# Gate stretch of a PEER layer: gathered rows a group later, weight copies behind the activation that frees their buffer, later splits behind a block's first product

## The chip, the cores and the metric

The program runs on one core of a Trainium2 chip. The metric is the device time of one execution in microseconds (us). Five engines of the core work side by side, each through its own queue in a fixed order: PE (matrix products; PEld is its weight load), DVE (vector work), ACT (activations and copies), POOL (here: indirect DMAs that gather table rows) and SP (it only issues DMAs). An engine waits at the head of its queue until what that instruction needs is there; nothing behind it can pass.

## The reference

Two layers over a sequence of 512 tokens of width 1024: a Griffin-like recurrent mixer in layer 0, latent attention in layer 1, and in both layers the same channel mixer, PEER, in which the change lies:

```python
def peer(h, w_q, sub_keys, u_tab, v_tab):
    q = (h @ w_q).reshape(B, S, PEER_HEADS, 2, PEER_HALF)
    s = jnp.einsum('bshpd,hpnd->bshpn', q, sub_keys)
    ...                                  # top 16 of 16 x 16 candidates per head
    idx = e1 * N_KEYS + e2               # 8 heads x 16 experts of 16384 per token
    g = jax.nn.softmax(cv, axis=-1)
    act = jax.nn.gelu(jnp.einsum('bcd,bchkd->bchk', hc, u_tab[ic]), approximate=False)
    return jnp.einsum('bchk,bchkd->bcd', gc * act, v_tab[ic])
```

## The kernel before

The 512 tokens are four blocks of 128. For the first three blocks (384 tokens) the kernel computes all 16384 experts densely and multiplies with a gate matrix that is zero where a token did not choose an expert. Only for the fourth block it gathers the 128 chosen rows per token one by one. Matrices in f32 are split into a high and a low part, and three products of the parts are added (`mm3`, lines 216 to 218).

Work comes in four kinds of pieces:

- A **u-part** (`u_part`, 128 in each layer, one per 128 experts): SP loads 512 KB of the u table (`raw`, four buffers), ACT copies it to `whi` (L179, three buffers), DVE subtracts to get `wlo` (L180), PE runs 24 products into one of two accumulator banks `u`, ACT applies the gelu (L1145 and L1140, `gact` or `gsp`) and, where `gsp` is written to memory, issues the store (L1141). The gelu is what frees the bank for the u-part after the next.
- A **gate group** (`gate_group`, 24 in each layer: 8 for each of three blocks, 16 tokens a group) is two half-groups. DVE makes two one-hot tensors `oo` (L1041) and the product `pr` of one of them with the gate (L1043, two buffers each); PE runs 16 products per half-group into `wps`; ACT copies `wps` to `stg` (L1052, two copies a half-group) and stores the group to `wscr` (L1054).
- A **gathered row** (`gather_steps`, 256 in each layer, in batches of 16 of the u table and then 16 of the v table): POOL gathers 512 KB into `grow` (four buffers), DVE makes a scalar product with it (L1487, `gdot`) or adds it to `gacc` (L1492).
- **Decoding** (`decode`, small `oh` work on DVE, some copies `ib` on ACT): it makes the gates of the next block, 7 steps in 8 groups.

After the choice of experts comes the **gate stretch**: 15 u-parts, and then 24 gate groups with some 2.5 u-parts for each group, and 74 gathered rows (`EARLY`) spread over groups 0 to 19. Then seven u-parts, and the products with the v table (`acc`), which read the gates back.

What stands where in a queue is settled when the program is built: a scheduler orders the instructions of all engines by a timeline of its own, unless the code says more. `issue_after(x)` says more: what the block issues on x's engine stands in the queue behind x. It adds no wait of its own, and it binds only instructions on that one engine. The loop that the change touches reads, before:

```python
for i in range(nt):
    more = 1 if i >= nsg and i % nsg < nsg // 2 else 0
    while state["u"] < n0 + (LEAD - UEND - n0) * (i + 1) // nt + more:
        u_part(after=wlast[-2])
    w, p = self.gate_group(pool, l, i // nsg, i % nsg, *prep[i // nsg])
    ...
    with tc.issue_after(plast[max(0, i - 1)]):
        while done < min(EARLY, EARLY * (i + 1) // (nt - QUIET)):
            next(gsteps)
            done += 1
```

Here `nt` is 24, `nsg` 8, `QUIET` 4 and `LEAD` 93.

Of the kernel before, what the change touches and what calls it, by code (L numbers as in the profile page):

```python
# [15 lines left out]
AF = mybir.ActivationFunctionType  # L16
OP = mybir.AluOpType
# [6 lines left out]
KC = D // P  # L24
# [15 lines left out]
ND = 3 * P  # L40
NSG = ND // TG
RING = 20
SPILL = 66
OWN = KC * T // ND
LEAD = OWN + RING - 3 + SPILL
# [3 lines left out]
QUIET = 4  # L49
EARLY = 74  # L50
# [5 lines left out]
GSCALE = 16384.0  # L56
# [27 lines left out]
class Trunk:  # L84
# [940 lines left out]
        nc.vector.tensor_tensor(gp[:, :, 1], gt, gp[:, :, 0], op=OP.subtract)  # L1025
        return et, gp

    def gate_group(self, pool, l, b, sg, et, gp):
        nc = self.nc
        shp = [P, 2, HT, P // 2, 2]  # L1030
        io = self.iota_e[:, 0].rearrange("p (e d) -> p e d", d=2).unsqueeze(1).unsqueeze(1).to_broadcast(shp)
        by_pair = "p q t (e d) -> p q t e d"
        stg = pool.tile([P, P, TG], F32, name="stg", bufs=2)
        for t0 in range(0, TG, HT):

            def toks(ap):
                return ap[:, (sg * TG + t0) // HT].unsqueeze(3).to_broadcast(shp)

            oo = pool.tile([P, 2, HT, P], F16, name="oo", bufs=2)
            pr = pool.tile([P, 2, HT, P], F16, name="pr", bufs=2)  # L1040
            nc.vector.tensor_tensor(oo.rearrange(by_pair, d=2), io, toks(et), op=OP.is_equal)  # L1041
            hot = oo[:, 0].rearrange("p t (e d) -> p t e d", d=2).unsqueeze(1).to_broadcast(shp)
            prod = nc.vector.tensor_tensor(pr.rearrange(by_pair, d=2), hot, toks(gp), op=OP.mult)  # L1043
            for a in range(0, HT, 4):
                wps = self.bank("wps")
                for t in range(4):
                    w = oo[:, 1, a + t]
                    out = wps[:, t * P:t * P + P]
                    lead = nc.tensor.matmul(out, w, pr[:, 0, a + t], start=True, stop=False).ins  # L1049
                    last = self.follow(lead, out, w, pr[:, 1, a + t], stop=True)  # L1050
                c = t0 + a
                nc.scalar.activation(stg[:, :, c:c + 4].rearrange("p e t -> p t e"),  # L1052
                                     wps.rearrange("p (t e) -> p t e", t=4), AF.Copy, scale=1.0 / GSCALE)
        nc.scalar.dma_start(self.wscr[l, b * (P // TG) + sg], stg.rearrange("p e t -> p (e t)"))  # L1054
        return last.ins, prod.ins

    def peer(self, l):
        nc, io, tc = self.nc, self.io, self.tc
        nd = NB - 1
        with ExitStack() as st:  # L1060
# [19 lines left out]
            with own:  # L1080
                for i, hs in enumerate(HALVES):
                    for k in range(KC):
# [5 lines left out]
                        hi, lo = (p[:, hs] for p in h[k])  # L1088
# [31 lines left out]
            gact, state = {}, {"u": 0}  # L1120

            def ring(t):
                held = (t - OWN) % RING < RING - 3
                return acts.tile([P, ND], F32, name="gact" if held else "gsp", bufs=RING - 3 if held else 3)

            nc.scalar.dma_start(self.xscr, self.x)

            def u_part(after=None, eng=None):
                t = state["u"]
                state["u"] = t + 1  # L1130
                out = self.bank("u", True)
                hi, lo = self.wtile(io["uT"][l][t], KC, eng=eng or nc.vector)
                with tc.issue_after(after) if after is not None else ExitStack():
                    for k, (bh, bl) in enumerate(h):
                        self.mm3(out[:, :ND], (hi[:, k, :], lo[:, k, :]), (bh[:, :ND], bl[:, :ND]), k == 0, k == KC - 1)
                if t < OWN:
                    gact[t] = self.x.rearrange("p k t -> p (k t)")[:, t * ND:t * ND + ND]
                elif LEAD - SPILL <= t < LEAD:
                    g = acts.tile([P, ND], F32, name="gsp", bufs=3)
                    nc.scalar.activation(g, out[:, :ND], AF.Gelu)  # L1140
                    nc.scalar.dma_start(self.gscr[l, t - (LEAD - SPILL)], g)  # L1141
                    return
                else:
                    gact[t] = ring(t)
                nc.scalar.activation(gact[t], out[:, :ND], AF.Gelu)  # L1145

            gpool = st.enter_context(tc.tile_pool(name=f"gath{l}", bufs=1))
            dec = st.enter_context(ExitStack())
# [5 lines left out]
            done = 0  # L1154
            total = 2 * P
            prep, gsel, gsteps = {}, [], None
            dpool = dec.enter_context(tc.tile_pool(name=f"dec{l}", bufs=1))

            def decodes(bs):
                for b in bs:  # L1160
                    res = []
                    for _ in self.decode(dpool, cvs[b], cis[b], iu[b], res):
                        yield
                    if b == nd:
                        gsel.append(self.gather_index(gpool, l, *res))
                    else:
                        prep[b] = self.gate_prep(pool, *res)

            with tc.tile_pool(name=f"pq{l}", bufs=1) as pool:
# [12 lines left out]
                for grp in range(4):  # L1182
# [7 lines left out]
                    for m in range(4):  # L1190
                        if m >= len(outs):
                            outs.append(self.bank("pq"))
                            with tc.issue_after(first) if first is not None else ExitStack():
                                w = self.wtile(io["w_pq"][wq + m], KC, eng=nc.gpsimd if grp else nc.vector)
                            self.lin(outs[m], w, h)
                        q = pool.tile([P, T], F32, name="pq_s", bufs=5)
                        nc.scalar.activation(q, outs[m], AF.Copy)
                        qs.append(q)
                    for b in (nd, *range(nd)):
# [4 lines left out]
                        for m in range(4):  # L1204
                            last = self.topk_half(pool, sc[:, m * P:m * P + P], vs[b][:, 4 * grp + m, :],
                                                  iu[b][:, 4 * grp + m, :])
# [9 lines left out]
            with tc.tile_pool(name=f"gate{l}", bufs=1) as pool:  # L1216
                nsg = P // TG
                steps = decodes(range(nd))
                for i in range(UDEC):
                    u_part()  # L1220
                while 0 not in prep:
                    next(steps)
                n0, nt = state["u"], nd * nsg
                ds = 0
                wlast, plast = [None, None], []
                for i in range(nt):
                    more = 1 if i >= nsg and i % nsg < nsg // 2 else 0
                    while state["u"] < n0 + (LEAD - UEND - n0) * (i + 1) // nt + more:
                        u_part(after=wlast[-2])
                    w, p = self.gate_group(pool, l, i // nsg, i % nsg, *prep[i // nsg])  # L1230
                    wlast.append(w)
                    plast.append(p)
                    while ds < 7 * (i + 2) // nsg:
                        next(steps, None)
                        ds += 1
                    with tc.issue_after(plast[max(0, i - 1)]):
                        while done < min(EARLY, EARLY * (i + 1) // (nt - QUIET)):
                            next(gsteps)
                            done += 1
                while state["u"] < LEAD:  # L1240
                    u_part(after=wlast[-1])
# [136 lines left out]
            for t, pair in held:  # L1378
                last = v_part(t, 0, *pair)
            self.preload(AF.Sqrt, emit(0))  # L1380
            rest, c = None, 0
            for q in range(2):
                for i, (t, pair) in enumerate(held):
                    with tc.issue_after(last):
                        last = v_part(t, 1, *pair, 2 * q * P, 2 * P, rest)
# [3 lines left out]
                    for _ in range((0, 2, 1, 1, 1, 0)[LAST * q + i]):  # L1389
                        with tc.issue_after(last):  # L1390
                            last = finish(c)
# [196 lines left out]
```

## Time and profile before

| What | us |
| --- | --- |
| median of 3 runs (2929.94 to 4088.32) | 2935.42 |
| the profiled execution | 2935.3 |
| its span, first to last instruction | 2933.5 |
| PE busy in the span | 2868.5 |
| DVE busy | 2469.5 |
| ACT busy | 1424.2 |
| POOL busy | 1104.4 |

The gate stretch of layer 0 runs from about 424 to 742 us of the span, that of layer 1 from about 1928 to 2246 us. The profile counts an engine as busy from an instruction's start to its modelled end, so a busy PE need not run at its peak; products that follow each other overlap, and their pace is read from their starts. In a line of the timeline the first number is the start, the second the duration, and the bracket at the end tells how long the engine was idle before it and what ended that wait.

### The profile page before, as it was taken

The page shows a single profiled execution, that of the slowest core. Times are in us where ns is not written, and L with a number is a line of the kernel's source. Part 1 is how long each engine was busy: PE and PEld are TensorE (multiplying, and loading weights), DVE is VectorE, ACT ScalarE, POOL GpSimd, SP SyncE. Part 2 cuts the span into 40 slices and gives each one's busy share as a digit, 9 for nine tenths or more (in the row PEclk, how much of TensorE's full clock was granted, in tenths as well). Part 3 has the DMA queues.
Part 4 walks back from the last instruction along what each step waited for, and adds up shares of the span by engine and source line. Part 5 has one row for each costly group of instructions (what it writes and reads, how often), then busy time and mean ns, then how long its engine had stood idle before and what let it go on. Part 6 is the DMA issues. An engine that isn't in the chain of part 4 may idle for free.

```text
span 2933.5 us, 43947 instructions
## 1 busy us (share of the span) xinstructions
PE 2868.5 (98%) x15680; PEld 2561.6 (87%) x15680; DVE 2469.5 (84%) x4717; ACT 1424.2 (49%) x2103; POOL 1104.4 (38%) x865
## 2 busy tenths in 40 slices
PE   7999999999999999999999999999999999999998
PEld 5688999999888889998778789999999888899997
DVE  8987899997988888879878877899986777888888
ACT  5754556665433333333576753556654333333333
POOL 4008715432232234535434446235321111245542
PEclk9999999999999999999999999999999999999999
DMA  8535559999999999999323343479999999999996
GB/s 314 189 137 186 169 179 370 355 368 339 327 372 360 367 315 354 322 348 324 113 87 130 122 137 124 138 282 356 369 344 335 314 330 317 317 329 353 349 334 218
DMA packets 296220, 813.71 MB, mean 277 GB/s; under 512 B 33153, under 2 KB 130561, under 8 KB 289601
## 3 DMA queue, kind: packets, MB, share of 16 engines
q1 hardware_dynamic: 188928, 439.41, 43.3%
q0 software_dynamic: 78912, 287.34, 27.5%
q10 hardware_dynamic: 28160, 84.14, 7.4%
q8 instruction: 124, 2.03, 0.3%
q14 instruction: 96, 0.78, 0.1%
HBM read 727.44 MB, written 83.36 MB: 276 GB/s over the span
## 4 chain that ended last, share of the span: by engine, by line
PE 85%; DVE 8%; ACT 3%; issue 2%; DMA 1%; POOL 1%; ACTq 0%; SPq 0%; DVEq 0%; POOLq 0%
PE acc L218 12%; PE acc L217 12%; PE acc L216 12%; PE u L216 11%; PE u L217 10%; PE u L218 10%; PE pq L216 2%; PE pq L217 2%; PE pq L218 2%; DVE wlo L180 2%; PE wps L1049 1%; PE wps L208 1%; PE sc L1202 1%; PE pv L849 1%; DVE ada_junk L153 1%
## 5 line engine op out<-in xcount | busy, mean ns | idle before, releaser
L216 PE MATMUL u<-h,wlo 128*128 128x384 f32 x2048 | 693.0, 338 | 7.3 <-ACT gsp L1140 5.9
L218 PE MATMUL u<-h,whi 128*128 128x384 f32 x2048 | 688.7, 336 | 0.0
L217 PE MATMUL u<-h,whi 128*128 128x384 f32 x2048 | 687.9, 336 | 0.0
L1483 POOL DMA_INDIRECT grow<-in_u_dram,idx x256 | 355.1, 1387 | 712.2 <-DVE gdot L1487 455.8
L218 PE MATMUL acc<-vh,ah 128*128 128x512 f32 x1512 | 589.5, 390 | 0.0
L217 PE MATMUL acc<-vl,ah 128*128 128x512 f32 x1512 | 589.2, 390 | 0.0
L1483 POOL DMA_INDIRECT grow<-in_v_dram,idx x256 | 373.5, 1459 | 546.3 <-DVE gacc L1492 357.4
L216 PE MATMUL acc<-vh,al 128*128 128x512 f32 x1512 | 551.1, 389 | 0.0
L179 ACT ACTIVATE whi<-raw 128x1024 fp32r<-128x1024 f32 (+2 forms) x362 | 352.8, 976 | 182.8 <-PE u L218 76.3
L180 DVE TENSOR_TENSOR vl<-vraw,vh 128x1024 fp32r<-128x1024 f32 x252 | 308.4, 1224 | 134.1 <-ACT vh L179 133.1
L180 DVE TENSOR_TENSOR wlo<-raw,whi 128x1024 fp32r<-128x1024 f32 x271 | 334.9, 1237 | 88.5 <-ACT whi L179 88.3
L216 PEld LDWEIGHTS u<-h,wlo 128*128 128x128 f32 x2048 | 386.2, 189 | 12.6 <-ACT gsp L1140 6.9
L217 PEld LDWEIGHTS u<-h,whi 128*128 128x128 f32 x2048 | 386.2, 189 | 2.8
L218 PEld LDWEIGHTS u<-h,whi 128*128 128x128 f32 x2048 | 385.9, 188 | 0.1
L218 PEld LDWEIGHTS acc<-vh,ah 128*128 128x128 f32 x1512 | 283.8, 188 | 59.2
L217 PEld LDWEIGHTS acc<-vl,ah 128*128 128x128 f32 x1512 | 283.7, 188 | 57.5
L216 PEld LDWEIGHTS acc<-vh,al 128*128 128x128 f32 x1512 | 283.8, 188 | 56.9
L1492 DVE SCALAR_TENSOR_TENSOR gacc<-grow,gdot,gacc 128x1024 f32<-128x1024 f32 x254 | 324.8, 1279 | 7.5 <-DMA grow<-in_v_dram,idx 6.4
L1487 DVE CUSTOM_DVE_ANT_0 grow<-grow,hn 128x1024 f32<-128x1024 f32 x256 | 309.4, 1219 | 17.0 <-DMA grow<-in_u_dram,idx 17.0
L179 ACT ACTIVATE vh<-vraw 128x1024 fp32r<-128x1024 f32 x252 | 264.5, 1050 | 107.8 <-issue 80.4
L179 ACT ACTIVATE ah<-gact 128x384 fp32r<-128x384 f32 x204 | 106.6, 522 | 388.0 <-PE acc L218 257.7
L1052 ACT ACTIVATE stg<-wps 128x512 f32<-128x512 f32 x192 | 187.3, 1116 | 48.0 <-PE wps L208 44.5
(421 smaller groups left out, 4510.6 us busy)
## 6 DMA issues: line engine op xcount, KB each, us to landing
raw<-in_uT_dram SPq DMA_DIRECT2D x256, 512.0 KB, 6.2
vraw<-in_v_dram SPq DMA_DIRECT2D x256, 512.0 KB, 6.2
wscr<-stg ACTq DMA_DIRECT2D x48, 1024.0 KB, 7.5
wt<-wscr SPq DMA_DIRECT2D x42, 1024.0 KB, 9.8
ada_raw<-in_adaw_dram SPq DMA_DIRECT2D x76, 512.0 KB, 4.1
gscr<-gsp ACTq DMA_DIRECT2D x132, 192.0 KB, 6.4
gact<-gscr SPq DMA_DIRECT2D x108, 192.0 KB, 6.5
ada_raw<-in_adaw_dram POOLq DMA_DIRECT2D x36, 512.0 KB, 6.3
```

The costliest lines, as they stand in the source:

```text
L153: nc.vector.tensor_tensor_reduce(junk, raw, self.csil, op0=OP.mult, op1=OP.add, scale=1.0, scalar=b, accum_out=col)
L179: last = nc.scalar.activation(hi, src, AF.Copy)
L180: lo = (eng or nc.vector).tensor_tensor(lo, src, hi.bitcast(F32), op=OP.subtract)
L208: return pe.add_instruction(mybir.InstMatmult(name=self.nc.get_next_instruction_name(), start_tensor_calc=start, stop_tensor_calc=stop, ld ...
L216: nc.tensor.matmul(out, al, bh, start=first, stop=False, **kw)
L217: nc.tensor.matmul(out, ah, bl, start=False, stop=False, **kw)
L218: last = nc.tensor.matmul(out, ah, bh, start=False, stop=last, **kw)
L849: self.last_pv = nc.tensor.matmul(ops, w, half, start=kb + n == 0, stop=kb + n == NB).ins
L1052: nc.scalar.activation(stg[:, :, c:c + 4].rearrange("p e t -> p t e"), wps.rearrange("p (t e) -> p t e", t=4), AF.Copy, scale=1.0 / GSCALE)
L1483: nc.gpsimd.indirect_dma_start(out=row, out_offset=None, in_=tabs[s], in_offset=bass.IndirectOffsetOnAxis(ap=idx[:, k:k + 1], axis=0))
L1487: nc.vector.tensor_tensor_reduce(row, row, hn, op0=OP.mult, op1=OP.add, scale=1.0, scalar=0.0, accum_out=col)
L1492: nc.vector.scalar_tensor_tensor(acc, row, col, acc, op0=OP.mult, op1=OP.add)
```

## The change

All four edits concern the order in the queues of the gate stretch; no instruction is added or taken away.

1. Gathered rows are traced from the second group on (`while i and`), and the 74 rows are spread over 19 groups and no longer over 20.
2. The copy to `whi` of u-part t stands, on ACT, behind the gelu of u-part t - 3. The three `whi` buffers go round, so the copy of t writes the buffer that the products of t - 3 read last.
3. The copies from `wps` to `stg` stand, on ACT, behind the gelu of the last u-part but one that was traced before the group.
4. The splits to `wlo` of the u-parts that are traced with the second group of a block stand, on DVE, behind the first product `pr` of that block.

```diff
-    def gate_group(self, pool, l, b, sg, et, gp):
+    def gate_group(self, pool, l, b, sg, et, gp, gelu):
...
-            prod = nc.vector.tensor_tensor(pr.rearrange(by_pair, d=2), hot, toks(gp), op=OP.mult)
+            prods.append(nc.vector.tensor_tensor(pr.rearrange(by_pair, d=2), hot, toks(gp), op=OP.mult).ins)
...
-                nc.scalar.activation(stg[:, :, c:c + 4].rearrange("p e t -> p t e"),
-                                     wps.rearrange("p (t e) -> p t e", t=4), AF.Copy, scale=1.0 / GSCALE)
+                with self.tc.issue_after(gelu):
+                    nc.scalar.activation(stg[:, :, c:c + 4].rearrange("p e t -> p t e"),
+                                         wps.rearrange("p (t e) -> p t e", t=4), AF.Copy, scale=1.0 / GSCALE)
...
-        return last.ins, prod.ins
+        return last.ins, prods[0], prods[1]
...
-                hi, lo = self.wtile(io["uT"][l][t], KC, eng=eng or nc.vector)
+                with ExitStack() as order:
+                    if LEAD - SPILL <= t < LEAD:
+                        order.enter_context(tc.issue_after(gelus[t - 3]))
+                    if prod is not None:
+                        order.enter_context(tc.issue_after(prod))
+                    hi, lo = self.wtile(io["uT"][l][t], KC, eng=eng or nc.vector)
...
-                        u_part(after=wlast[-2])
-                    w, p = self.gate_group(pool, l, i // nsg, i % nsg, *prep[i // nsg])
+                        u_part(after=wlast[-2], prod=firsts[-1] if i % nsg == 1 else None)
+                    w, q, p = self.gate_group(pool, l, i // nsg, i % nsg, *prep[i // nsg], gelus[-2])
                     wlast.append(w)
+                    firsts.append(q)
                     plast.append(p)
...
-                        while done < min(EARLY, EARLY * (i + 1) // (nt - QUIET)):
+                        while i and done < min(EARLY, EARLY * i // (nt - QUIET - 1)):
```

The order that the scheduler makes of it differs from before in the gate stretch and the first steps after it; POOL's queue is the same. Three places follow.

**DVE, layer 0, where the second group is made ready.** Before, `pr_4433` and `pr_4457` are the two products of the second group, and each `grow` row a scalar product with a gathered row:

```order
L1006 TENSOR_TENSOR e0_4351<-oh_4654 128x64
L1487 ISA grow_4493,gdot_4352<-grow_4493,hn_1627 128x1024
L1487 ISA gdot_4352 128x1
L1487 ISA grow_4496,gdot_4352<-grow_4496,hn_1627 128x1024
L1487 ISA gdot_4352 128x1
L1487 ISA grow_4499,gdot_4352<-grow_4499,hn_1627 128x1024
L1487 ISA gdot_4352 128x1
L1043 TENSOR_TENSOR pr_4433<-oo_4432,gp_4209 128x2048
L180 TENSOR_TENSOR wlo_4573<-raw_4571,whi_4572 128x1024
L1043 TENSOR_TENSOR pr_4457<-oo_4456,gp_4209 128x2048
```

Of the change, `pr_4422` and `pr_4446` are the same two products:

```order
L180 TENSOR_TENSOR wlo_4493<-raw_4491,whi_4492 128x1024
L1042 TENSOR_TENSOR oo_4445<-iota_e_83,et_4204 128x2048
L1006 TENSOR_TENSOR e0_4351<-oh_4642 128x64
L180 TENSOR_TENSOR wlo_4527<-raw_4525,whi_4526 128x1024
L1044 TENSOR_TENSOR pr_4422<-oo_4421,gp_4209 128x2048
L1044 TENSOR_TENSOR pr_4446<-oo_4445,gp_4209 128x2048
L1497 ISA grow_4652,gdot_4479<-grow_4652,hn_1627 128x1024
L1497 ISA gdot_4479 128x1
L997 TENSOR_TENSOR oh_4782<-iota_m_85,rc_4344 128x1024
L1497 ISA grow_4655,gdot_4479<-grow_4655,hn_1627 128x1024
```

Seven gathered rows stood ahead of the second group's first product before; now three do, and the fourth to seventh stand behind both products.

**ACT, layer 0, at the end of the stretch.** Before, `whi_7858` and `whi_7892` are the copies of u-parts 88 and 89, and `gsp_7701`, `gsp_7735` and `gsp_7819` the gelus of u-parts 84, 85 and 86:

```order
L1140 ACTIVATE gsp_7701<-u_7670 128x384
L1141 DMA gscr_93<-gsp_7701 128x384
L179 ACTIVATE whi_7858<-raw_7857 128x1024
L179 ACTIVATE whi_7892<-raw_7891 128x1024
L1140 ACTIVATE gsp_7735<-u_7704 128x384
L1141 DMA gscr_93<-gsp_7735 128x384
L1140 ACTIVATE gsp_7819<-u_7788 128x384
```

Of the change, with the last `stg` copies between:

```order
L1149 ACTIVATE gsp_7735<-u_7704 128x384
L1150 DMA gscr_93<-gsp_7701 128x384
L1054 ACTIVATE stg_7738<-wps_7777 128x4x128
L179 ACTIVATE whi_7858<-raw_7857 128x1024
L1150 DMA gscr_93<-gsp_7735 128x384
L1056 DMA wscr_96<-stg_7738 128x2048
L1149 ACTIVATE gsp_7819<-u_7788 128x384
L1150 DMA gscr_93<-gsp_7819 128x384
L179 ACTIVATE whi_7892<-raw_7891 128x1024
```

The gelu of u-part 85 stood behind the copies of 88 and 89; now each copy stands behind the gelu three u-parts earlier.

**DVE, layer 0, fourth group of the second block.** Before, `pr_6029` and `pr_6053` are the two products of that group (half-groups 22 and 23), and `wlo_6243` is the split of u-part 59:

```order
L1041 TENSOR_TENSOR oo_6028<-iota_e_83,et_5109 128x2048
L1041 TENSOR_TENSOR oo_6052<-iota_e_83,et_5109 128x2048
L1004 TENSOR_TENSOR oh_5941<-oh_5941 128x4x32
L180 TENSOR_TENSOR wlo_6243<-raw_6241,whi_6242 128x1024
L1043 TENSOR_TENSOR pr_6029<-oo_6028,gp_5114 128x2048
L1043 TENSOR_TENSOR pr_6053<-oo_6052,gp_5114 128x2048
```

Of the change, from `pr_6023` to `pr_6047`, the same two products, with `wlo_6237` the split of u-part 59:

```order
L1044 TENSOR_TENSOR pr_6023<-oo_6022,gp_5103 128x2048
L1497 ISA grow_5780,gdot_4479<-grow_5780,hn_1627 128x1024
L1497 ISA gdot_4479 128x1
L1042 TENSOR_TENSOR oo_6046<-iota_e_83,et_5098 128x2048
L1004 TENSOR_TENSOR oh_5935<-oh_5935 128x4x32
L180 TENSOR_TENSOR wlo_6237<-raw_6235,whi_6236 128x1024
L1497 ISA grow_5944,gdot_4479<-grow_5944,hn_1627 128x1024
L1497 ISA gdot_4479 128x1
L1044 TENSOR_TENSOR pr_6047<-oo_6046,gp_5103 128x2048
```

Before, both products stood behind the split; now the first stands ahead of it, and two gathered rows, a one-hot tensor and the split stand between the two products.

More of the change, by code (lines that the diff above doesn't have):

```diff
@@ L1033, in gate_group @@
         stg = pool.tile([P, P, TG], F32, name="stg", bufs=2)
+        prods = []
         for t0 in range(0, TG, HT):
@@ L1126, in peer, with u_part @@
             nc.scalar.dma_start(self.xscr, self.x)
-            def u_part(after=None, eng=None):
+            gelus = []
+            def u_part(after=None, eng=None, prod=None):
                 t = state["u"]
@@ L1139, in u_part @@
                     g = acts.tile([P, ND], F32, name="gsp", bufs=3)
-                    nc.scalar.activation(g, out[:, :ND], AF.Gelu)
+                    gelus.append(nc.scalar.activation(g, out[:, :ND], AF.Gelu).ins)
                     nc.scalar.dma_start(self.gscr[l, t - (LEAD - SPILL)], g)
@@ L1144, in u_part @@
                     gact[t] = ring(t)
-                nc.scalar.activation(gact[t], out[:, :ND], AF.Gelu)
+                gelus.append(nc.scalar.activation(gact[t], out[:, :ND], AF.Gelu).ins)
             gpool = st.enter_context(tc.tile_pool(name=f"gath{l}", bufs=1))
@@ L1224, in peer @@
                 ds = 0
-                wlast, plast = [None, None], []
+                wlast, plast, firsts = [None, None], [], []
                 for i in range(nt):
```

## The prediction

> **What bounds the kernel now.** I read the busy times and the chain first.
>
> ```profile
> PE 2868.5 (98%) x15680; PEld 2561.6 (87%) x15680; DVE 2469.5 (84%) x4717; ACT 1424.2 (49%) x2103; POOL 1104.4 (38%) x865
> PE 85%; DVE 8%; ACT 3%; issue 2%; DMA 1%; POOL 1%; ACTq 0%; SPq 0%; DVEq 0%; POOLq 0%
> ```
>
> PE is idle for 2933.5 - 2868.5 = 65 us in the whole span, and an edit that only reorders queues can win no more than such waits and what follows from them. The next view is who waited for whom, for PE, in the two gate stretches (424 to 742 us, and then 1928 to 2246 us; columns: total us, times, longest).
>
> ```profile
> PE wps L1049 <- DVE pr L1043: 4.4, 4, 2.0
> PE u L216 <- ACT gsp L1140: 1.5, 1, 1.5
> PE u L216 <- DVE wlo L180: 0.2, 1, 0.2
> ...
> PE u L216 <- ACT gsp L1140: 4.4, 3, 1.8
> PE wps L1049 <- DVE pr L1043: 4.0, 1, 4.0
> PE u L216 <- DVE wlo L180: 0.2, 1, 0.2
> ```
>
> Layer 0 loses 4.4 + 1.5 + 0.2 = 6.1 us, layer 1 loses 4.4 + 4.0 + 0.2 = 8.6 us, together **14.7 us**. To each wait I add what it does to PE's pace, from the timeline:
>
> ```profile
> 450.52 0.33 PE L216 MATMUL u<-h,wlo 128*128 128x384 f32 x1
> 451.91 0.34 PE L218 MATMUL u<-h,whi 128*128 128x384 f32 x1
> ...
> 445.16 0.22 PE L1049 MATMUL wps<-pr,oo 128*128 128x128 f16 x1 [2.04 <-DVE pr L1043]
> 446.00 0.24 PE L208 MATMUL wps<-pr,oo 128*128 128x128 f16 x1
> 446.39 0.66 PE L216 MATMUL u<-h,wlo 128*128 128x384 f32 x1 [0.16 <-DVE wlo L180]
> 449.62 0.34 PE L217 MATMUL u<-h,whi 128*128 128x384 f32 x1
> ...
> 1948.26 0.66 PE L216 MATMUL u<-h,wlo 128*128 128x384 f32 x1 [0.15 <-DVE wlo L180]
> 1951.49 0.34 PE L217 MATMUL u<-h,whi 128*128 128x384 f32 x1
> ...
> 2192.42 0.44 PE L216 MATMUL u<-h,wlo 128*128 128x384 f32 x1 [1.85 <-ACT gsp L1140]
> 2193.58 0.41 PE L216 MATMUL u<-h,wlo 128*128 128x384 f32 x1
> 2197.23 0.34 PE L216 MATMUL u<-h,wlo 128*128 128x384 f32 x1
> ```
>
> The first two rows are eight products apart: 1.39 / 8 = 0.174 us a product, so 24 x 0.174 = 4.2 us a u-part; sixteen `wps` products take 16 x 0.84 / 15 = 0.9 us. From 446.39 to 449.62 lie ten products, which took 3.23 us and not 1.74: 1.5 us lost to a slower pace after the wait. The same ten stand at 1948.26 (1.5 us), and from 2193.58 to 2197.23 twelve took 3.65 us and not 2.09 (1.6 us). These half-pace stretches cost **4.6 us**. So 14.7 + 4.6 = 19.3 us is all there is to win.
>
> [...]
>
> **The change part by part.** *The gathered rows.* The longest waits, 2.0 and 4.0 us, have this cause on DVE (first 424 to 450 us, then 1925 to 1955 us), with the landing times of all gathers beside it:
>
> ```profile
> DVE grow L1487 <- DMA grow<-in_u_dram,idx: 2.5, 1, 2.5
> ...
> DVE grow L1487 <- DMA grow<-in_u_dram,idx: 4.5, 1, 4.5
> ...
> DMA to landing us min/median/max: 4.4/7.5/13.6
> ```
>
> A row gathered late held up DVE's queue, and the product `pr` of the second group stood behind it. In the new order both products of that group stand ahead of the fourth row, and the rows that must be fetched afresh (the fifth on, since four buffers were filled early) come after them. I take both waits and both half-pace stretches as gone: 2.0 + 0.2 + 1.5 + 4.0 + 0.2 + 1.5 = 9.4 us. Rows and their DMAs only come later: 3 after the second group where 7 were asked before, and 74 after group 19 in both, so at no group has the new order asked DVE, POOL or the DMA queues for more than before.
>
> *The weight copies.* The wait of PE at 720.79:
>
> ```profile
> 719.31 1.06 ACT L179 ACTIVATE whi<-raw 128x1024 fp32r<-128x1024 f32 x1 [3.10 <-PE u L218]
> 720.27 0.47 ACT L1140 ACTIVATE gsp<-u 128x384 f32<-128x384 f32 x1
> ...
> 720.79 0.44 PE L216 MATMUL u<-h,wlo 128*128 128x384 f32 x1 [1.52 <-ACT gsp L1140]
> ```
>
> The copy for u-part 89 waits for the products of 86 to free its buffer, and the gelu of 85, ready 4.2 us earlier, stands behind it; u-part 87 needs the bank that this gelu frees. With the gelu of t - 3 ahead of the copy of t this can't happen. Layer 1 has three such places. All four go: 1.5 + 4.4 + 1.6 (half-pace stretch) = 7.5 us. The price is that a copy starts one gelu (0.5 us) later; its split is done about 0.5 + 1.0 + 1.2 = 2.7 us after u-part t - 3, and PE asks for it two u-parts, 8.3 us, after that u-part's end. Hidden.
>
> *The `stg` copies.* Four of them take 3.85 us:
>
> ```profile
> 430.00 3.85 ACT L1052 ACTIVATE stg<-wps 128x512 f32<-128x512 f32 x4
> ```
>
> At the end of the stretch a gelu may still stand behind up to four, at most 0.5 + 4 x 1.0 + 0.5 = 5 us after its products, where PE asks after two half-groups and a u-part: 1.8 + 4.2 = 6 us. Nothing.
>
> *The first product of a block.* At the start of layer 0's stretch:
>
> ```profile
> 418.09 0.65 ACT L1019 ACTIVATE et<-et 128x256 f16<-128x256 f32 x2
> 419.67 2.35 DVE L1041 TENSOR_TENSOR oo<-iota_e,et 128x2048 f16<-128x2048 f16 x2
> 426.05 2.31 DVE L1043 TENSOR_TENSOR pr<-oo,gp 128x2048 f16<-128x2048 f16 x2
> 424.14 0.33 PE L216 MATMUL u<-h,wlo 128*128 128x384 f32 x1
> ```
>
> The first group's products now stand after u-part 28 on PE, at 424.1, and on DVE ahead of the splits of 29 and 30. From 418.8, `oo` twice (2.3), small work (1.3) and `pr` twice (2.3) end at 423.5 and 424.7, and the split of 29 at 425.8; PE asks at 424.1, 425.0 and 425.9. It fits by 0.1; layer 1 has 0.3 us more of small work. Between 0 and 0.5 a layer; I take 0.3 in all.
>
> *The fourth group of the second block.* Here DVE is the tight engine:
>
> ```profile
> 450.00:500.00 50.00, 49.60 (x376) 48.55 (x375) 50.00 (x66) 30.34 (x38) 27.64 (x14) 1.00 0.98 358
> 500.00:550.00 50.00, 50.00 (x363) 49.53 (x360) 47.90 (x55) 34.11 (x44) 25.69 (x12) 1.00 0.99 360
> 550.00:600.00 50.00, 48.72 (x387) 47.12 (x386) 48.18 (x65) 32.72 (x41) 20.14 (x14) 1.00 0.96 351
> ...
> L180 DVE TENSOR_TENSOR wlo<-raw,whi 128x1024 fp32r<-128x1024 f32 x30 | 36.4, 1215 | 3.9 <-ACT whi L179 3.9
> L1492 DVE SCALAR_TENSOR_TENSOR gacc<-grow,gdot,gacc 128x1024 f32<-128x1024 f32 x15 | 19.1, 1274 | 0.0
> ...
> 569.77 1.22 DVE L180 TENSOR_TENSOR wlo<-raw,whi 128x1024 fp32r<-128x1024 f32 x1 [1.82 <-ACT whi L179]
> 570.91 2.35 DVE L1043 TENSOR_TENSOR pr<-oo,gp 128x2048 f16<-128x2048 f16 x2
> ```
>
> Columns of the windows: length, busy us of PE, PEld, DVE (third), ACT, POOL, clock, DMA share, GB/s: DVE works 146.1 of 150 us. From start to start a large DVE instruction takes 1.14 us (569.77 to 570.91). At 569.77 a split that waited for its copy stood ahead of both products, and PE waited 1.2 us. Now the first product goes ahead. Call the end of u-part 55 zero. The split of 57 ends no earlier than 2.4 us before it (its copy stands behind the gelu of 54); then a row, `oo`, a product, a row and small work (2.4), split 58 (3.5), first product (4.7), row, `oo`, small work (7.1), split 59 (8.2), row (9.4), second product 10.5. PE reaches it after two u-parts and two half-groups: 8.3 + 1.8 = 10.1. Late by **0.4**; in layer 1, where a little more stands between, by 0.6.
>
> *What is left over.* Counted off the orders from the first group to the thirteenth's first product, DVE has 100 large instructions at 1.14, 16 `gacc` at 1.19 and 13 us of small work (146.1 less the large ones in those windows): 146 us, against 30.75 u-parts and 22 half-groups, 148 us, on PE; before it was 147 against 146. So DVE keeps up by 2 us, and a wait of it for a row or a copy shows on PE. Bounds: 0, and two waits as long as those seen (2.0 + 1.5 and 4.0 + 1.5) = 9. I take **2.5**, the shorter DVE wait for a row.
>
> Sum: 19.3 - 0.3 - 1.0 - 2.5 = 15.5 us. From the profiled execution's 2935.3, which is the median to 0.1: **2920**.
>
> **The rivals.** *Late rows take it back.* The DMA share is 0.96 to 0.99, gathers land after 4.4 to 13.6 us, and the rows come a little denser (74 over 19 groups). Each late row cost 2.0 or 4.0 us and a half-pace stretch, 4.5 on average; 74 rows are four and a half batches a layer, and three more late ones among the nine batches make 13.5 and 2933. Against it: DVE's waits from 420 to 760 us hold just the one wait for a row, at this share, and the total asked at any group is not higher.
>
> *The gelu still comes late.* If the `stg` copies ahead of it start a microsecond later than I count, the four waits for `gsp` stay: 1.5 + 4.4 + 1.6 = 7.5 back, 2927. For it: the margin is 1 us at two groups a layer.
>
> *Slower: the copies behind the gelus starve DVE.* Each copy starts 0.5 us later. If DVE's splits met their copies on arrival, 32 u-parts x 0.5 = 16 us of idle DVE a layer, less the 2 us to spare, would be 14 on PE, 28 in both, with three half-pace stretches of 1.5 on top: 2935.3 - 19.3 + 32.5 = 2948. It decides from 39 late splits on (19.3 / 0.5). For it: DVE already waits for copies from 420 to 760 us:
>
> ```profile
> DVE wlo L180 <- ACT whi L179: 20.8, 18, 3.5
> ```
>
> Against: those are waits of an engine that ran ahead, and the buffers leave it 8.3 - 2.7 us.
>
> **How the numbers follow.** Forecast 0.58 (2916 with no loss left, 2926 with the last one at its upper bound), late gelu 0.10, late rows 0.22 (2928 to 2937), slower 0.10. The range 2912 to 2937 leaves out the last; below it goes 4 us past 2916, since one of the runs shown took 2929.94 and not the median. Two per cent, 59 us, is about what a measurement can tell from no change here; none of the cases reaches it on either side, since all waits and half-pace stretches together are 19 us, so within 2% has 0.96, with 0.03 for slower and 0.01 for faster left to what I haven't seen.
>
> **What would show it.** Right: PE's waits on `pr` in 424 to 450 and 1928 to 1955 gone, no wait for `gsp`, no half-pace stretch there, a wait of under 1 us near the fourth group of block two, and each stretch 6 to 9 us shorter. Wrong: `grow` waits of DVE in the middle of a stretch (late rows); `gsp` rows behind `stg` with PE idle (late gelu); DVE waits for `whi` well above the 20.8 us with PE waiting for `wlo` (slower); or a stretch that gets shorter while the `acc` stage behind it gets longer.

## The result, and the profile after

The change takes 2917.47 us in the median of six runs (2915.03 to 2923.60), against 2936.14 us before in the same session. The ratio is **0.9948, 95% interval 0.9939 to 0.9958**, a gain of 15.3 us (0.0052 x 2936; 12.3 to 17.9): under 2 per cent, and well outside the noise. The medians lie further apart, 18.7 us: one of the six runs of before took 4088.32 us, in a slow state, and the ratio is that of the means of the other runs (2918.85 to 2934.19). The forecast was 2920, a gain of 15.5. The profiled execution of after took 2922.16 us, its span 2920.4.

The busy times and the chain of the page of after:

```profile
PE 2866.0 (98%) x15680; PEld 2559.3 (88%) x15680; DVE 2465.9 (84%) x4717; ACT 1424.4 (49%) x2103; POOL 1100.1 (38%) x865
PE 90%; DVE 5%; ACT 2%; issue 2%; DMA 1%; POOL 0%; SPq 0%; ACTq 0%; DVEq 0%; POOLq 0%
```

PE's idle time is 2920.4 - 2866.0 = 54 us, where it was 65, and DVE's share of the chain fell from 8% to 5%. PE's waits in the two gate stretches of after, first layer 0 and then layer 1 (columns: total us, times, longest):

```profile
PE wps L1050 <- DVE pr L1044: 1.1, 1, 1.1
...
PE wps L1050 <- DVE pr L1044: 1.1, 1, 1.1
```

These two rows stand where six stood before. No wait for `gsp` is left, the waits for `pr` at the second group are gone, and behind neither wait does PE run at half pace (the granted clock was 1.00 throughout both stretches): 14.7 us of waits have become 2.2, and 4.6 us of half pace have become none.

The length of a stretch I read from the start of the gelu of u-part 27 to that of u-part 96, in the timeline of ACT. That reaches some 340 us into the `acc` stage; PE waits nowhere in that part, before or after, so the difference is made in the gate stretch. Four rows of before, then the same four of after:

```profile
422.79 0.49 ACT L1140 ACTIVATE gsp<-u 128x384 f32<-128x384 f32 x1
1085.38 0.49 ACT L1145 ACTIVATE gact<-u 128x384 f32<-128x384 f32 x1 [3.07 <-PE u L218]
1922.05 0.49 ACT L1140 ACTIVATE gsp<-u 128x384 f32<-128x384 f32 x1
2592.50 0.49 ACT L1145 ACTIVATE gact<-u 128x384 f32<-128x384 f32 x1 [3.07 <-PE u L218]
```

```profile
418.54 0.49 ACT L1149 ACTIVATE gsp<-u 128x384 f32<-128x384 f32 x1
1074.27 0.49 ACT L1154 ACTIVATE gact<-u 128x384 f32<-128x384 f32 x1 [3.07 <-PE u L218]
1920.46 0.49 ACT L1149 ACTIVATE gsp<-u 128x384 f32<-128x384 f32 x1
2579.36 0.49 ACT L1154 ACTIVATE gact<-u 128x384 f32<-128x384 f32 x1 [3.07 <-PE u L218]
```

Layer 0: 662.6 us before, 655.7 after. Layer 1: 670.5 and 658.9. The stretches gained 6.9 + 11.6 = **18.4 us**, 3 more than the forecast has for the whole. But from 1085.38 to 1922.05 there are 836.7 us, and in after, from 1074.27 to 1920.46, 846.2: **9.5 us given back** between the layers, where no instruction was meant to move. (The remaining 4.2 us lie ahead of the first stretch; 4.4 of them are there by the gelu of u-part 12, up to which the order is unchanged, so that is scatter.)

The first part of the 9.5 us is found at the end of layer 0, in the timelines of DVE and PE. Before:

```profile
1409.57 0.69 DVE L1365 COPY onat<-acc 128x512 f32<-128x512 f32 x1 [0.37 <-PE acc L218]
1410.17 2.60 DVE L1492 SCALAR_TENSOR_TENSOR gacc<-grow,gdot,gacc 128x1024 f32<-128x1024 f32 x2
...
1412.83 0.33 PE L1373 MATMUL ot<-ident,gacc 128*128 128x128 f32 x1
```

After:

```profile
1398.46 0.69 DVE L1375 COPY onat<-acc 128x512 f32<-128x512 f32 x1 [0.37 <-PE acc L218]
1399.07 2.60 DVE L1502 SCALAR_TENSOR_TENSOR gacc<-grow,gdot,gacc 128x1024 f32<-128x1024 f32 x2
1404.60 1.28 DVE L1502 SCALAR_TENSOR_TENSOR gacc<-grow,gdot,gacc 128x1024 f32<-128x1024 f32 x1 [2.94 <-DMA grow<-in_v_dram,idx]
...
1405.94 0.48 PE L1383 MATMUL ot<-ident,gacc 128*128 128x128 f32 x1 [4.36 <-DVE gacc L1502]
```

Before, **two** gathered rows stand behind the copy of the accumulator (`onat`); after, **three**. The third lands late, DVE waits 2.94 us for it, and PE 4.36 us for DVE. The program order of DVE shows the same: in layer 0's `acc` stage the rows stand one to three steps of the stage later than before, from its first row on, and at its end still one. In layer 1's the two orders agree.

### The profile page after: what moved, and what is told of

The parts are those of the page before. It is cut to its first block, busy times and chain, and to the rows that moved or that the text cites. A ratio compares the mean times of both kernels' runs of the same rounds, so it can differ in the third digit from the quotient of the medians.

```text
span 2920.4 us, 43994 instructions
## 1 busy us (share of the span) xinstructions
PE 2866.0 (98%) x15680; PEld 2559.3 (88%) x15680; DVE 2465.9 (84%) x4717; ACT 1424.4 (49%) x2103; POOL 1100.1 (38%) x865
## 4 chain that ended last, share of the span: by engine, by line
PE 90%; DVE 5%; ACT 2%; issue 2%; DMA 1%; POOL 0%; SPq 0%; ACTq 0%; DVEq 0%; POOLq 0%
PE u L216 12%; PE u L218 12%; PE u L217 12%; PE acc L217 12%; PE acc L218 12%; PE acc L216 12%; PE pq L216 2%; PE pq L217 2%; PE pq L218 2%; PE wps L1050 1%; PE wps L208 1%; PE sc L1211 1%; PE pv L849 1%; DVE wlo L180 1%; PE tp L830 1%
```

## The experiments

Diffs are against the change, except where a kernel is told to keep an edit alone. All ratios are against the kernel before, run on the same chip in the same session. Stretch lengths are from one profile each. In layer 1 they repeat well (658.9 us in two profiles of the change, and 658.9 or 659.0 in three other kernels with edits 1 and 2); in layer 0 two profiles of one kernel differed by 0.8 us (the change) and 1.2 us (weight 0.5, below).

**Without edit 1**

```diff
-while i and done < min(EARLY, EARLY * i // (nt - QUIET - 1)):
+while done < min(EARLY, EARLY * (i + 1) // (nt - QUIET)):
```

> The change without edit 1: rows traced from the first group on, over 20 groups, as before; edits 2, 3 and 4 stay. Theory (each edit removes its own waits): PE waits for the product pr of the second group come back, about 2.0 us in layer 0 and 4.0 us in layer 1, with a half-pace stretch of about 1.5 us behind each, and no wait for gsp. At the end of layer 0's acc stage only two rows stand behind the last copy out of the accumulators, as before (three in the change), so the 4.4 us wait for the last row there is gone. 2917.5 + 9.4, less up to 6 for the end of layer 0: 2921 to 2927. Rival (any reordering of this size helps, the edits are interchangeable): no pr wait at the second group, 2915 to 2918.

Measured: 2924.96 us, ratio 0.9974 (0.9964 to 0.9984); stretches 6.5 us shorter than before, so 12 of the 18.4 are lost. The size was as expected, the place was not wholly. The longest waits in the timeline of PE were

```profile
424.49 0.41 PE L216 MATMUL u<-h,wlo 128*128 128x384 f32 x1 [3.08 <-DVE wlo L180]
450.10 0.41 PE L216 MATMUL u<-h,wlo 128*128 128x384 f32 x1 [1.70 <-DVE wlo L180]
...
1926.69 0.41 PE L216 MATMUL u<-h,wlo 128*128 128x384 f32 x1 [3.03 <-DVE wlo L180]
```

The waits for `pr` at the second group that I had expected, 2.0 and 4.0 us, are only 0.74 and 0.97 us. The splits now wait for the block's first product (edit 4) and for three rows that stand ahead of them on DVE. So edit 4 is only as cheap as forecast (0.3 us) because edit 1 has moved the rows out of its way. No wait at the end of layer 0, where two rows are left. The rival, that any reordering helps as much, falls.

**Without edit 2**

```diff
-if LEAD - SPILL <= t < LEAD:
-    order.enter_context(tc.issue_after(gelus[t - 3]))
```

> The change without edit 2: the weight copies are not held behind the gelu three u-parts earlier; edits 1, 3 and 4 stay. Theory: PE's waits for gsp come back at the end of the stretches, 1.5 us in layer 0 and up to 4.4 us in layer 1 with 1.6 us at half pace, and no wait for pr at the second group. The end of layer 0 has two rows behind the last copy, as before, so no wait there. 2917.5 + 7.5, less up to 6: 2919 to 2925. Rival (edit 3 alone, the stg copies, already moves the gelus ahead): no gsp wait, 2912 to 2917.

Measured: 2917.79 us, ratio 0.9957 (0.9944 to 0.9971); stretches 13.8 us shorter than before. PE's waits for `gsp` are back:

```profile
718.95 0.44 PE L216 MATMUL u<-h,wlo 128*128 128x384 f32 x1 [1.52 <-ACT gsp L1147]
724.93 0.44 PE L216 MATMUL u<-h,wlo 128*128 128x384 f32 x1 [1.52 <-ACT gsp L1147]
...
2217.40 0.44 PE L216 MATMUL u<-h,wlo 128*128 128x384 f32 x1 [1.53 <-ACT gsp L1147]
```

4.6 us where I had expected 7.5, in other places than before. Counted off the order of ACT, each wait is where the copy for u-part t stands ahead of the gelu of t - 4, and not only of that of t - 3: twice in layer 0, once in layer 1. At the end of layer 0 two rows are left and no wait. By the ratios this kernel gains 2.7 to 2.9 us less than the change, and the intervals overlap: what edit 2 gives in the stretches (4.6 us) and what the end of layer 0 takes from the change are nearly of one size.

**Without edit 4**

```diff
-u_part(after=wlast[-2], prod=firsts[-1] if i % nsg == 1 else None)
+u_part(after=wlast[-2], prod=None)
```

> The change without edit 4: the splits of a block's second group are not held behind the block's first product; edits 1, 2 and 3 stay. Theory: edit 4 is worth little. Either a short wait for pr (0 to 2 us) shows at the first or second group of a block, in place of the 1.1 us wait at the second half of the fourth group of block two, which comes from rows and a split between the pair's products and not from edit 4. 2916 to 2922. Rival (edit 4 makes the 1.1 us waits by pulling the products apart): both waits gone, 2 us less than the change.

Measured: 2921.45 us, ratio 0.9963 (0.9950 to 0.9976); stretches 17.7 us shorter. The wait in block two is halved but not gone:

```profile
562.89 0.23 PE L1050 MATMUL wps<-pr,oo 128*128 128x128 f16 x1 [0.52 <-DVE pr L1044]
2055.86 0.23 PE L1050 MATMUL wps<-pr,oo 128*128 128x128 f16 x1 [0.51 <-DVE pr L1044]
2157.79 0.23 PE L1050 MATMUL wps<-pr,oo 128*128 128x128 f16 x1 [0.80 <-DVE pr L1044]
```

With it, other short waits come, and the sum is what it was. Edit 4 makes about half of the 1.1 us waits and gives nothing that is clear of the scatter. At the end of layer 0 three rows are left, and PE waits 2.8 us.

**Rows earlier in layer 0's `acc` stage, weight 1.0**

```diff
-plan = ((KC, 0.2), (36, (0.95, 0.6)[l]), ...
+plan = ((KC, (1.0, 0.2)[l]), (36, (0.95, 0.6)[l]), ...
```

> The change, with one number of the row plan of layer 0's acc stage raised (the weight of its first eight steps, 0.2 to 1.0), so that fewer rows are left at its end: one behind the last copy out of the accumulators instead of three. Theory: the 4.4 us wait for the last row and the half-pace stretch behind it (some 6 us with what follows directly) are an effect of the row that the change left over there; with it gone the profiled execution falls from 2922.2 to 2913 to 2916, and the median from 2917.5 to 2912 to 2916. Rival (the wait is a matter of when one gather happens to land): the wait stays at 2 us or more, and the median stays within 1.5 us of the change. Other rival (rows early in the acc stage hold up DVE there): new PE waits between 745 and 780 us, 2918 or more.

Measured: 2917.66 us, ratio 0.9946 (0.9933 to 0.9959); profiled 2917.66. The wait at the end is gone (no row at all was left behind the copy there, where I had expected one), and the profiled execution fell by 4.5 us, not by 6 to 9. A new wait stands at the start of the `acc` stage, behind two rows on DVE:

```profile
734.58 1.22 DVE L1497 CUSTOM_DVE_ANT_0 grow<-grow,hn 128x1024 f32<-128x1024 f32 x1
736.19 1.22 DVE L1497 CUSTOM_DVE_ANT_0 grow<-grow,hn 128x1024 f32<-128x1024 f32 x1
...
738.59 0.47 PE L216 MATMUL acc<-vh,al 128*128 128x512 f32 x1 [1.89 <-issue]
```

The split `al` of the first gated activation ends at 738.5, behind them. Both theories were right in part: the end is freed, and the start pays for it, a little ahead of the 745 to 780 us that the other rival named. The median is no lower than the change's.

**The change again**

> The change itself, beside the experiments. In its first profile PE waited 4.4 us at the end of layer 0 for the last gathered row, and the part from there to layer 1's stretch took 9.5 us more than before, while both stretches together took 18.4 us less. Theory: the wait comes from the row order, so it is there again, 2 to 5 us. Rival (chance of one landing): no wait there, and the part as long as before. Ratio to before 0.994 to 0.996.

No edit. Measured: 2917.47 us, ratio 0.9947 (0.9932 to 0.9962); stretches 19.3 us shorter. The wait is there again, of another size:

```profile
1403.43 1.28 DVE L1502 SCALAR_TENSOR_TENSOR gacc<-grow,gdot,gacc 128x1024 f32<-128x1024 f32 x1 [0.69 <-DMA grow<-in_v_dram,idx]
...
1404.78 0.33 PE L1383 MATMUL ot<-ident,gacc 128*128 128x128 f32 x1 [2.10 <-DVE gacc L1502]
```

From layer 0's gelu 96 to the first gelu of layer 1 it took 648.7 us, where before had 645.2 and the first profile of the change 654.7. So the wait is there both times, and the 9.5 us of the first profile were a bad draw: besides the wait of 4.36 us, PE ran 30.7 us of that part at half clock, against 13.7 in before and 20.5 here (the last section has what the windows show of this).

**Rows earlier in layer 0's `acc` stage, weight 0.5**

```diff
-plan = ((KC, 0.2), (36, (0.95, 0.6)[l]), ...
+plan = ((KC, (0.5, 0.2)[l]), (36, (0.95, 0.6)[l]), ...
```

> The change, with the weight of the first eight steps of layer 0's acc stage at 0.5 (0.2 in the change, 1.0 in the last experiment on it): one row behind the last copy out of the accumulators, three in the change; at the start of the acc stage one row stands ahead of the first split of the gated activations, two with 1.0, none in the change. Theory: no wait at the end of layer 0, and the 1.9 us wait of PE at the start of the acc stage that the weight of 1.0 brought is at most 0.9; 2 to 6 us below the change of the same call. Rival: the row ahead of the first split costs what the end gives, within 1.5 us of the change.

Measured: 2913.62 us, ratio 0.9939 (0.9925 to 0.9952). One row is left at the end, and PE waits neither there nor at the start of the `acc` stage:

```profile
1398.42 0.69 DVE L1375 COPY onat<-acc 128x512 f32<-128x512 f32 x1 [0.37 <-PE acc L218]
1399.03 1.28 DVE L1502 SCALAR_TENSOR_TENSOR gacc<-grow,gdot,gacc 128x1024 f32<-128x1024 f32 x1
...
1401.39 0.27 PE L1383 MATMUL ot<-ident,gacc 128*128 128x128 f32 x1
```

The same kernel once more:

> The change with the weight of 0.5 in layer 0's acc stage once more, to narrow its interval. Theory: no wait at the end of layer 0, 2 to 5 us below the change (ratio to before 0.9925 to 0.994, where the change had 0.9947 and 0.9948). Rival: no better than the change, 0.9945 or more.

2913.89 us, ratio 0.9935 (0.9922 to 0.9948). Both medians lie 3.6 to 3.9 us under the change's, by the ratios 2.3 to 3.8 us, and the wait is gone in both profiles. It beats the kernel before beyond doubt; against the change the intervals overlap, so by the times alone the gain is likely, not shown.

**Edit 1 alone** (edits 2, 3 and 4 undone)

```diff
 # against the kernel before
-while done < min(EARLY, EARLY * (i + 1) // (nt - QUIET)):
+while i and done < min(EARLY, EARLY * i // (nt - QUIET - 1)):
```

> Only edit 1: gathered rows from the second group on; the other three edits undone. Theory (edits 1 and 2 add up): no wait for pr over 1.2 us at the second group, waits for gsp as before (1.5 us in layer 0, up to 4.4 us in layer 1). Both stretches together 9 to 13 us shorter than before, 2923 to 2928 where before is 2936. Rival (edit 1 needs the split behind the first product): the wait at the second group stays at 2 us or more and the stretches gain under 6 us.

Measured: 2931.16 us, ratio **1.0002** (0.9991 to 1.0013); stretches only 5.2 us shorter. The waits for `pr` at the second group are gone as the theory says. But there are more and longer ones for `gsp` than before, in the waits of layer 0's stretch, then of layer 1's:

```profile
PE u L216 <- ACT gsp L1146: 4.2, 3, 1.5
...
PE u L216 <- ACT gsp L1146: 5.1, 4, 2.4
```

9.3 us against 5.9, and in layer 1 PE also waits 1.1 us for a copy `vh` at the start of the `acc` stage, where it did not wait before. The timeline of ACT and PE shows the longest wait for `gsp`:

```profile
2205.84 1.06 ACT L179 ACTIVATE whi<-raw 128x1024 fp32r<-128x1024 f32 x1 [2.06 <-PE u L218]
2206.80 1.94 ACT L1053 ACTIVATE stg<-wps 128x512 f32<-128x512 f32 x2
2208.54 0.52 ACT L1146 ACTIVATE gsp<-u 128x384 f32<-128x384 f32 x1
...
2209.11 0.44 PE L216 MATMUL u<-h,wlo 128*128 128x384 f32 x1 [2.40 <-ACT gsp L1146]
```

A copy that had to wait for its buffer, and two `stg` copies, stand ahead of the gelu. Moving rows on DVE made the scheduler order ACT anew, and worse. My theory that the edits add up falls.

**Edit 2 alone** (edits 1, 3 and 4 undone)

```diff
 # against the kernel before
+if LEAD - SPILL <= t < LEAD:
+    order.enter_context(tc.issue_after(gelus[t - 3]))
```

> Only edit 2: the weight copies behind the gelu three u-parts earlier; the other three undone. Theory: no wait for gsp at the end of a stretch, waits for pr at the second group as before (2.0 and 4.0 us, half pace behind each). Both stretches together 4 to 8 us shorter than before, 2928 to 2932 where before is 2936. Rival (the copies starve DVE when the rows stand early): DVE waits for whi well above 20.8 us in the stretch of layer 0, PE waits for wlo, no gain.

Measured: 2928.66 us, ratio 0.9987 (0.9975 to 0.9999); stretches 6.6 us shorter, as expected. One wait of 0.7 us for `gsp` is left, in layer 1, behind four `stg` copies, and the waits for `pr` at the second group stand (3.04 and 4.11 us, together 1.1 us more than before). DVE waited 17.7 us for copies in layer 0's stretch, 20.8 before: the copies starve nothing, and the rival falls.

**Edits 1 and 2 together** (3 and 4 undone)

```diff
 # against the kernel before: the two diffs above
```

> Edits 1 and 2 together, 3 and 4 undone. Edit 1 alone shortened both stretches by 5.2 us, edit 2 alone by 6.6, the four together by 18.5. Theory: the two need each other, and edits 3 and 4 add nothing: no wait for gsp, no wait for pr over 1 us, both stretches 16.5 to 18.5 us shorter than before, a wait of 2 to 4 us at the end of layer 0 (three rows are left there), ratio to before 0.994 to 0.997. Rival (edit 3 carries what is above the sum): both stretches about 11.8 us shorter.

Measured: 2918.59 us, ratio 0.9953 (0.9938 to 0.9967); stretches **18.7 us** shorter, all that the four edits give. The waits of over 0.3 us that are left in the stretches and at the end of layer 0:

```profile
563.48 0.23 PE L1050 MATMUL wps<-pr,oo 128*128 128x128 f16 x1 [0.51 <-DVE pr L1044]
1403.94 0.33 PE L1382 MATMUL ot<-ident,gacc 128*128 128x128 f32 x1 [2.62 <-DVE gacc L1501]
2063.11 0.23 PE L1050 MATMUL wps<-pr,oo 128*128 128x128 f16 x1 [0.52 <-DVE pr L1044]
```

5.2 and 6.6 alone, 18.7 together: alone, each edit lets the other's waits grow, edit 1 those for `gsp` by 3.4 us, edit 2 those for `pr` at the second group by 1.1 us.

**Edits 1 and 3** (2 and 4 undone)

```diff
 # against edit 1 alone
+with self.tc.issue_after(gelu):
     nc.scalar.activation(stg[:, :, c:c + 4].rearrange("p e t -> p t e"), ...
```

> Edits 1 and 3, with 2 and 4 undone. Theory: in every kernel so far PE waited for gsp where a copy of u-part t stands, on ACT, ahead of the gelu of t - 4 as well, with 0.9 to 2.4 us for each such place: 1 and 3 waits before, 3 and 3 with edit 1 alone, 2 and 1 without edit 2, none with edit 2. This kernel has 4 such places in layer 0 and 6 in layer 1: ten waits, 12 to 16 us in all, both stretches as long as before or longer (within 3 us of it). Rival (the stg copies behind the gelu free the gelu, so that edit 3 stands in for edit 2): both stretches 12 us or more shorter.

Measured: 2927.35 us, ratio 0.9987 (0.9978 to 0.9996); stretches 7.2 us shorter. Both numbers missed. The places counted off the order (4 and 6) gave 4 and 5 waits, so the rule finds them to within one, but a wait cost 0.9 us on average and not 1.2 to 1.6. With edit 3 no `stg` copy stands ahead of the gelu, which fits, and the longest wait is 1.5 us, not 2.4:

```profile
PE u L216 <- ACT gsp L1147: 3.9, 4, 1.5
...
PE u L216 <- ACT gsp L1147: 4.0, 5, 1.5
```

Edit 3 does not stand in for edit 2. It makes the same fault cheaper. The rule does not find every wait for `gsp`: with edit 2 alone and without edit 1 there is no such place, and PE waited 0.7 and 0.6 us once; the wait of 1.0 us that before has in layer 1 stands behind a `stg` copy, not behind such a place.

**Without edit 3**

```diff
-with self.tc.issue_after(gelu):
-    nc.scalar.activation(stg[:, :, c:c + 4].rearrange("p e t -> p t e"), ...
+nc.scalar.activation(stg[:, :, c:c + 4].rearrange("p e t -> p t e"), ...
```

> The change without edit 3. Theory: nothing changes in the stretches (the gelus already stand ahead by edit 2): one wait of 1.1 us for pr in each layer, both stretches 17.5 to 19.5 us shorter than before, ratio to before 0.994 to 0.996. Rival (edit 3 has a part of its own): new waits for gsp, stretches gain under 15 us.

Measured: 2916.86 us, ratio 0.9953 (0.9939 to 0.9967); stretches 18.4 us shorter, waits as in the change. With edits 1 and 2 there, edit 3 does nothing.

**All kernels in one table.** "Stretches" is what both stretches gained on before in the profile, "measured" is (1 - ratio) x 2933, "rows left" counts the gathered rows behind the copy `onat`, "wait" is PE's behind them.

| kernel | stretches, us | rows left | wait, us | measured gain, us |
| --- | --- | --- | --- | --- |
| change, its two sessions | 18.4, 19.3 | 3 | 4.4, 2.1 | 15.3, 15.5 |
| without edit 3 | 18.4 | 3 | 2.4 | 13.8 |
| without edit 4 | 17.7 | 3 | 2.8 | 10.9 |
| edits 1 and 2 | 18.7 | 3 | 2.6 | 13.8 |
| edits 1 and 3 | 7.2 | 3 | 3.3 | 3.8 |
| edit 1 | 5.2 | 3 | 3.0 | -0.6 |
| edit 2 | 6.6 | 3 | 3.3 | 3.8 |
| without edit 1 | 6.5 | 2 | none | 7.6 |
| without edit 2 | 13.8 | 2 | none | 12.6 |
| weight 1.0 | 17.0 | 0 | none | 15.8 |
| weight 0.5, its two sessions | 18.0, 19.3 | 1 | none | 17.9, 19.1 |

Three rows left: a wait in eight profiles of eight, 2.1 to 4.4 us. Two or fewer: none in six (before among them). The measured gain lies below that of the stretches by 2.8 to 6.8 us, 4.4 on average, where three rows are left, and by 0.3 on average where fewer are. Each measured gain is uncertain by 3 to 4 us either way, so only the averages count. The profiles give the same size without the times: from layer 0's gelu 96 to layer 1's first gelu it took 649.5 us on average with three rows left and 645.7 with fewer. So the end of layer 0 takes back **about 4 us**, the wait of some 3 us and what PE loses in pace behind it (in the first profile of the change the granted clock was 0.50 from 1403.72 to 1410.55 us).

Which edit leaves the third row there is not shown: edit 1 alone and edit 2 alone each leave three, while the change without edit 1 and the change without edit 2 each leave two.

## Why the prediction was right

The time came out 2.5 us under the forecast, and the gain by the ratio 0.2 us under it, but that closeness is luck: two errors offset each other. The stretches gave 3 to 4 us more than the sum, and the end of layer 0, which the sum leaves out, took about 4 back.

- **What there was to win, 19.3 us**: right to within some 2 us. In the change 14.7 us of waits became 2.2 and the three half-pace stretches are gone, half-pace stretches behind the waits of 2.04 and 1.85 us among them. That makes 17.1 us, where the stretches gained 18.4 and 19.3; the 1.3 to 2.2 us more are not accounted for. No run took more than 19.3 us out of the stretches.
- **Rows 9.4, copies 7.5**: the sum holds, the split between edits does not. Alone the edits gave 5.2 and 6.6 us, with the other one there 12.1 (18.7 - 6.6) and 13.5 (18.7 - 5.2). I had costed each by the waits it names, in the order of before; but each edit also changes what the scheduler puts elsewhere. One of layer 1's three waits for `gsp`, the 1.0 us, did not have the cause that I gave all three.
- **`stg` copies, nothing**: right beside edit 2 (18.4 us without edit 3; with edit 2 alone 0.7 us were left behind `stg` copies). **First product, 0.3**: no wait there in the change, but only since edit 1 clears DVE's queue (3.08 and 3.03 us without it).
- **Fourth group of block two, 0.4 and 0.6**: the place was right, the size was not: 1.07 and 1.08 us. The two products of the group start, on DVE, at

```profile
557.70 1.22 DVE L1044 TENSOR_TENSOR pr<-oo,gp 128x2048 f16<-128x2048 f16 x1
...
563.53 1.22 DVE L1044 TENSOR_TENSOR pr<-oo,gp 128x2048 f16<-128x2048 f16 x1
```

5.8 us apart, as summed (10.5 less 4.7). So it is what stands ahead of them that came late: u-part 55 ended at 553.5, and the split of 57 at 551.8, 1.7 us earlier and not 2.4.
- **Left over, 2.5 us**: this step failed. I took it that a DVE wait for a late row shows on PE. In layer 0 the same row as before, the seventh, still landed late, and DVE waited 1.73 us for it:

```profile
440.94 1.23 DVE L1497 CUSTOM_DVE_ANT_0 grow<-grow,hn 128x1024 f32<-128x1024 f32 x1 [1.73 <-DMA grow<-in_u_dram,idx]
```

PE did not wait for anything there: both products of the second group now stood ahead of that row. Nothing else was left in either stretch.
- **The end of layer 0, not in the sum at all**: this is the step that is missing. I stopped following the rows where the stretch ends, with 74 asked for in both orders, and took the rest for unchanged; the order of DVE is not unchanged. I had named the sign of it (a stretch that gets shorter while what is behind it gets longer), without a price. It took back about 4 us.

Sum by the runs: 18.4 to 19.3, less about 4, is 14.4 to 15.3; 15.3 and 15.5 were measured. Two per cent is not the least that such a measurement can tell: here 0.5 per cent came out with an interval of 0.1 on each side. Of the rivals, *late gelu* has no trace in the change, *late rows* cost PE nothing in the stretch, for all that DVE waited once, but showed at the very end of the layer, and *copies starve DVE* is refuted: DVE waited 11.5 us for copies in layer 0's stretch, less than the 20.8 of before:

```profile
DVE wlo L180 <- ACT whi L179: 11.5, 8, 4.2
```

## What to carry to other kernels

Where a scheduler orders the queues, an edit that only moves instructions is to be followed in the order to the end of the phase, on every engine: rows that stood one to three steps later from the end of the stretch on came due 660 us later, at the one place that waits for the last row. Two waits of one stretch are best removed together before either is judged: here one edit alone measured 1.0002, the other 0.9987, and the pair 0.9953. A rule on a queue (no copy ahead of the gelu of t - 4) can be counted in the program order, and finds most of the places; what each place costs has still to be measured.

## What the runs showed of the hardware

In these runs the length of PE's wait did not tell whether its pace fell behind the wait. Before, ten or twelve products at half pace followed waits of 2.04 and 1.85 us. Without edit 1, the products behind a wait of 3.08 us went on at 0.17 us each, so it cost its length alone. Two windows of before, then two of the kernel without edit 1 (after the length comes PE's busy time; the third number from the end is the granted clock):

```profile
442.66:446.07 3.41, 1.37 (x19) 1.12 (x17) 3.33 (x4) 1.05 (x2) 1.68 (x1) 1.00 1.04 417
446.07:449.48 3.41, 3.25 (x13) 3.12 (x11) 3.41 (x5) 2.38 (x3) 0.00 (x0) 0.50 1.03 405
...
419.92:423.33 3.41, 1.49 (x27) 1.31 (x24) 3.41 (x8) 3.41 (x5) 2.04 (x2) 1.00 0.16 58
423.33:426.74 3.41, 2.25 (x13) 2.28 (x14) 3.41 (x6) 1.38 (x2) 2.66 (x2) 1.00 0.94 231
```

The first ten products at half pace lie in the second of these windows, at a granted clock of 0.50; the ten from 1948.26 and the twelve from 2193.58 lie, to 0.2 us, in 1947.93:1951.35 and 2193.69:2197.11, at 0.50 as well. So half pace was half clock. In the profiles of before and after the clock's records hold only 1.00 and 0.50. Within each of the two the stretches at 0.50 begin whole multiples of 3.4133 us apart, to within 0.03 us, and all but the one at the very end last 3.413 us or twice that; the waits between them did not shift this spacing. A window here is the 3.413 us from one such multiple to the next. The wait of 2.04 us lay in one window, which left PE busy for 1.37 us of it, and half clock followed; the wait of 3.08 us lay across the last two rows above, with 1.49 and 2.25 us of busy PE, and none followed. In the gate stretches of before half clock followed three windows, with 1.37, 0.90 and 1.56 us of busy PE (from 442.66, 1944.52 and 2190.28), and none with 1.88 or more. Outside them busy time alone does not sort the windows: in before, half clock followed one with 2.95 us of busy PE (from 1422.28) and did not follow one with 1.64 (from 1528.09). What sets the clock is not shown.

Three times in the gate stretches of before, a wait cost 1.5 or 1.6 us on top of its length, with half clock behind it. Time at half clock differs from profile to profile, and with it the length. From layer 0's gelu 96 to layer 1's first gelu the fourteen profiles took 643.1 to 654.7 us, with 10.2 to 30.7 us of it at half clock. A least-squares fit to the fourteen, an estimate from these lengths, the waits in the table and the times at half clock, gives 0.98 us for each us that PE waits behind the gathered rows and 0.39 us for each us at half clock, and leaves at most 1.1 us open in any of them. At the start of the program it explains less: the gelu of u-part 12, up to which the order is the same in all these kernels, started between 353.0 and 358.7 us; the two latest had 13.7 us at half clock by then, the others 3.4 to 10.2.
